# RWKV keys left unnormalised: the inverse squared norm moves into the inversion of the 32x32 blocks

## The chip, the cores and the metric

The kernel runs on one core of one Trainium2 chip. The metric is device time in microseconds (us) of one execution. A core has a matrix engine (TensorE; PE in the profile, with its weight loads shown apart as PEld), a vector engine (VectorE, DVE), a scalar engine (ScalarE, ACT), a general engine (GpSimd, POOL) and SyncE (SP), which here only issues transfers. Transfers are issued by SP and by ACT. Each engine works through its own instructions in a fixed order, so an instruction that waits holds up everything behind it on that engine.

## The reference

The model has two layers on 1024 tokens of width 1024: an even layer (a gated mixer) and an odd layer (RWKV-7 time mixing), each followed by a SwiGLU feed-forward block (FFN). The change lies in the odd layer. What matters of it, cut:

```python
kk = heads(k * k_k)                                   # 16 heads of 64
kk = kk / jnp.maximum(jnp.sqrt(jnp.sum(kk * kk, axis=-1, keepdims=True)), 1e-12)
k = k * (1 + (a - 1) * k_a)
y = wkv7_scan(rh, decay, kh, vh, -kk, kk * ah)
...
def step(state, inp):                                 # one token
    r_t, w_t, k_t, v_t, a_t, b_t = inp                # a_t = -kk, b_t = kk * a
    sa = jnp.einsum('bhvk,bhk->bhv', state, a_t)
    state = (state * w_t[:, :, None, :] + sa[..., None] * b_t[:, :, None, :]
             + v_t[..., None] * k_t[:, :, None, :])
    return state, jnp.einsum('bhvk,bhk->bhv', state, r_t)
```

So each head's key vector `kk` is divided by its length before it enters the recurrence, once as `-kk` and once as `kk * a`.

## The kernel before, in words

Dense products. Every large product is made of three products in a reduced 32-bit format: weights and activations are split into a high and a low part (`split`, L156: ScalarE copies the high part, L157; VectorE subtracts, L158), and `mm3` (L398) multiplies high by high, low by high and high by low into one PSUM tile of 128x512 (L399, L400, L401). "A dense product" below is one of these three. Small products (norms, bonus, interactions, transposes) are made in full 32-bit floats. The tokens are treated in two halves of 512.

The odd layer of a half goes through two stages that concern us.

**Projections** (`project`, L1184). A loop runs over 8 pairs of heads (`p`). For each pair: the 24 dense products of `k`; the decay and learning-rate products (L1291, L1292) with their tanh on ScalarE; the 24 dense products of `r`, among which small products are placed (`small`, L1319). `norms` (L1313) is four products of the squared keys with a two-column indicator (L1314), which leave the squared norms of 512 tokens in columns of the PSUM tile `bo`; then VectorE (L1316) and GpSimd (`rsqrt`, L404) turn them into inverse norms `rn`. After the `r` products, eight products of `rn` with the identity (L1333) spread the inverse norms over the partitions into `rb`, and VectorE multiplies `k * k_k` by it (L1339) to get `kkn`. From `kkn` come `ar` and `bk`, which are stored to DRAM. One pair later, `interact` (L1233) makes 16 products of `bk` with `ar` (L1238), stores their 32x32 diagonal blocks to `at_d`, and after pairs 3 and 7 loads the blocks of four pairs as `iat` (L1253). `bonus` (L1259) adds four small products per pair (L1260).

**Inversion** (`invert`, L1402). For four pairs at once, with one block per partition, VectorE runs 31 steps of two instructions (L1413, L1418) on `xi`, which starts as the identity (L1407, L1408 on GpSimd), then copies (L1420) and stores it to `xi_d` (L1422). The steps are interleaved with the pair loop and with the products of `v` that follow it (L1385 to L1387). A half has two inversions; the second uses the same tiles as the first.

**Recurrence** (`recur`, L1440) of 8 chunks of 64 tokens, emitted beside FFN products that fill TensorE meanwhile (`drive`, L1019). After every second chunk `turn_out` (L1678) transposes the result on TensorE (L1460 from `ysb`), VectorE multiplies it by the gate (L1691), and it is stored to `y_d` (L1694). `take_act` loads `y_d` in four pieces on ScalarE's queue (L121), splits each into `ahi` and `alo`, and `out_proj` (L1726) multiplies them by the output weights.

Order. The program is built with a scheduler (`schedule_with_timeline_sim=True`, L2034): the order of each engine's instructions is fixed when the kernel is built, by a simulated timeline of the whole program with priorities for the recurrence. A small change in one stage therefore moves instructions in those behind it.

PSUM has 8 banks. In the projections they are 3 for dense products, 4 `aux` (for `zw`, `za`, the interactions and `rb`) and 1 `bo` (`PROJ`, L392).

Of the kernel before, what the change touches and what calls it, by code (L numbers as in the profile page):

```python
# [9 lines left out]
F32 = mybir.dt.float32  # L10
# [33 lines left out]
def tile_trunk(  # L44
# [347 lines left out]
    PROJ = {"mm": ("mm", 3), "aux": ("aux", 4), "bo": ("bo", 1)}  # L392
# [10 lines left out]
    def rsqrt(t):  # L403
        pool.tensor_tensor(out=t, in0=t, in1=mhalf[:, : t.shape[1]], op=ALU.pow)  # L404
# [640 lines left out]
    xi_d = [dram.tile([2, 8, 2, 8, 32, 2, 32], F32, name=f"xi_d{h}") for h in range(2)]  # L1045
    at_d = [dram.tile([2, 8, 2, 8, 32, 32], F32, name=f"at_d{h}") for h in range(2)]
# [137 lines left out]
    def project(h, hn1, kp, ring, keep, before_v):  # L1184
# [3 lines left out]
        def tmp(tag, bufs=1, shape=None, dt=F32):  # L1188
            if early.get(tag):
                return early[tag].pop(0)  # L1190
            return ep.tile(shape or [P, HT], dt, tag=tag, bufs=bufs, name=tag)
# [34 lines left out]
        ind2 = tmp("ind2", 1, [P, 2])  # L1226
        pool.memset(ind2, 0.0)
        pool.memset(ind2[0:64, 0:1], 1.0)
        pool.memset(ind2[64:128, 1:2], 1.0)
# [3 lines left out]
        def interact(p, ar, bk):  # L1233

            oa = auxt()
            for c in range(8):
                for r in range(2):
                    pe.matmul(  # L1238
                        oa[rows[r], c * 64 : (c + 1) * 64], bk[rows[r], c, 0, :], ar[rows[r], c, 0, :],
                        start=True, stop=True,  # L1240
                    )
            at = tmp("kkn", 2)
            act.activation(at, oa, AF.Copy)
            for r in range(2):
                for q in range(2):
                    b0 = r * 64 + q * 32
                    sp.dma_start(
                        at_d[h][q, p, r].rearrange("c s t -> s c t"), c64(at)[b0 : b0 + 32, :, q * 32 : q * 32 + 32]
                    )
            if p % 4 == 3:  # L1250
                iat = tmp("iat", 1, [P, 32, 32])
                for q in range(2):
                    sp.dma_start(  # L1253
                        iat[q * 64 : q * 64 + 64].rearrange("b s t -> b (s t)"),
                        at_d[h][q, p - 3 : p + 1].rearrange("p r c s t -> (p r c) (s t)"),
                    )
                return iat
# [19 lines left out]
        for p in range(KT):  # L1277
# [32 lines left out]
            n2 = bo[:, 64 + 8 * p : 72 + 8 * p]  # L1310
            rn = tmp("rn", 2, [P, 4, 2, 8])[:, 0, 0, :]

            def norms(j):  # L1313
                pe.matmul(n2[:, 2 * j : 2 * j + 2], sq[:, j * P : (j + 1) * P], ind2, start=True, stop=True)  # L1314
                if j == 3:
                    dve.tensor_scalar(out=rn, in0=n2[:, 0:8], scalar1=1e-24, scalar2=None, op0=ALU.max)  # L1316
                    rsqrt(rn)

            small = [lambda j=j: norms(j) for j in range(4)]  # L1319
# [10 lines left out]
            rb = auxt()  # L1330
            for j in range(4):
                for r in range(2):
                    pe.matmul(  # L1333
                        rb[rows[r], j * P : (j + 1) * P], bc(rn[:, 2 * j + r : 2 * j + r + 1], [P, 64]), ident,
                        start=True, stop=True,
                    )
            ar, bk = tmp("ar", 2, [P, 8, 2, 64]), tmp("bk", 2, [P, 8, 2, 64])
            kkn = tmp("kkn", 2)
            dve.scalar_tensor_tensor(out=kkn, in0=kt, scalar=col(C_KK + p), in1=rb, op0=ALU.mult, op1=ALU.mult)  # L1339
# [23 lines left out]
        bs = tmp("rn", 2, [P, 4, 2, 8])  # L1363
# [10 lines left out]
        for cb in range(2):  # L1374
            os_ = [(mmt, auxt)[(j + 2 * cb) // 2 % 2]() for j in range(4)]
# [26 lines left out]
    def invert(h, p0, iat, tmp):  # L1402
# [5 lines left out]
        pool.memset(xf[:, 0:2048:65], 1.0)  # L1408
# [629 lines left out]
```

## Time and profile before

| | |
|---|---|
| median of 3 runs | 2454.44 us (2453.6 to 2456.31) |
| span of the profiled execution | 2450.8 us |
| what lies between that span and the median of the runs | 3.6 us |
| TensorE busy | 2369.0 us (97%), 15567 records |
| VectorE, ScalarE, GpSimd busy | 1476.8 us (60%), 935.9 us (38%), 217.1 us (9%) |
| granted TensorE clock, mean | 0.989 |
| projections of half 0, half 1 | about 846 to 1034 us, 1414 to 1610 us |
| recurrence of half 0, half 1 | about 1060 to 1262 us, from about 1626 us on |

The profile was taken on one execution of its own; its span from the first to the last instruction is the base for sums. Its whole time is not listed separately, so a sum is carried to the runs by the 3.6 us. In the timeline a row gives start, duration, engine, line, operation, output and inputs, and how many like instructions were merged. A row of TensorE lasts longer than the distance to the next row, because products are pipelined: the cost of one is read from start to start. A 32-bit float product appears as two records, so a group of four such products reads "x8".

### The profile page before, as it was taken

What the parts mean: (1) busy time and instruction counts of PE and PEld (TensorE: products, weight loads), DVE (VectorE), ACT (ScalarE), POOL (GpSimd) and SP (SyncE); (2) the same over time, 40 slices, a digit from 0 to 9 for tenths busy, and PEclk for the clock granted to TensorE, in tenths of its full rate; (3) what the DMA queues carried; (4) which work ended last, traced back from release to release, by engine and by line L of the source; (5) the groups of instructions that cost most, each with busy time, mean ns of one, the idle gap of its engine ahead of it and who ended that gap; (6) DMA issues with size and microseconds to landing.
All of it is one profiled execution on the core that took longest, in us unless ns stands there. A gap on an engine that the chain in (4) does not pass through costs nothing. (4 is left out here: it accounts for less than half of the span.)

```text
span 2450.8 us, 38190 instructions
## 1 busy us (share of the span) xinstructions
PE 2369.0 (97%) x15567; PEld 1945.9 (79%) x15567; DVE 1476.8 (60%) x2328; ACT 935.9 (38%) x1403; POOL 217.1 (9%) x246
## 2 busy tenths in 40 slices
PE   8999999999899999999999999999999999999998
PEld 6888888888687788778777678777888788888887
DVE  6445766655558758856767947856664446434443
ACT  6233444443114644422335744433232324322223
POOL 0200000000000033101100133201100001000001
PEclk9999999999999999999999999999999999999999
DMA  5114443334655554774435465675433422433231
GB/s 177 52 60 140 153 146 103 113 103 155 252 203 204 165 149 131 226 212 132 129 126 155 160 166 141 186 223 158 143 112 122 129 78 90 150 105 95 86 103 52
DMA packets 406767, 342.17 MB, mean 140 GB/s; under 512 B 78080, under 2 KB 351616, under 8 KB 405824
## 3 DMA queue, kind: packets, MB, share of 16 engines
q10 hardware_dynamic: 266048, 195.33, 26.3%
q1 hardware_dynamic: 140544, 144.41, 18.8%
q8 instruction: 122, 2.00, 0.3%
q14 instruction: 53, 0.43, 0.0%
HBM read 263.07 MB, written 76.61 MB: 139 GB/s over the span
## 5 line engine op out<-in xcount | busy, mean ns | idle before, releaser
L399 PE MATMUL mm<-ahi,whi 128*128 128x512 f32 x1376 | 541.0, 394 | 5.8 <-DVE h L493 3.7
L400 PE MATMUL mm<-alo,whi 128*128 128x512 f32 x1376 | 541.5, 394 | 1.1 <-DVE alo L158 1.1
L401 PE MATMUL mm<-ahi,wlo 128*128 128x512 f32 x1376 | 540.1, 393 | 1.4 <-DVE wlo L158 1.4
L157 ACT ACTIVATE whi<-raw 128x1024 fp32r<-128x1024 f32 (+1 forms) x280 | 282.0, 1013 | 557.4 <-PE mm L400 428.6
L158 DVE TENSOR_TENSOR wlo<-raw,whi 128x1024 fp32r<-128x1024 f32 (+1 forms) x280 | 328.4, 1177 | 246.5 <-ACT whi L157 231.0
L399 PEld LDWEIGHTS mm<-ahi,whi 128*128 128x128 f32 x1376 | 259.0, 188 | 63.1 <-ACT whi L157 6.2
L401 PEld LDWEIGHTS mm<-ahi,wlo 128*128 128x128 f32 x1376 | 259.2, 188 | 58.4 <-DVE wlo L158 2.7
L400 PEld LDWEIGHTS mm<-alo,whi 128*128 128x128 f32 x1376 | 259.3, 188 | 57.7 <-issue 2.5
L493 DVE TENSOR_TENSOR h<-h,mm 128x512 f32<-128x512 f32 x276 | 185.5, 684 | 162.5 <-PE mm L401 161.6
L399 PE MATMUL mm<-hidhi,wdhi 128*128 128x512 f32 x304 | 117.5, 395 | 2.9 <-ACT hidhi L958 2.3
L400 PE MATMUL mm<-hidlo,wdhi 128*128 128x512 f32 x304 | 119.7, 394 | 0.0
L401 PE MATMUL mm<-hidhi,wdlo 128*128 128x512 f32 x304 | 119.0, 391 | 0.0
L730 PE MATMUL mm<-ahi,whi 128*128 128x512 f32 x296 | 115.6, 390 | 0.0
L731 PE MATMUL mm<-alo,whi 128*128 128x512 f32 x296 | 115.2, 389 | 0.0
L732 PE MATMUL mm<-ahi,wlo 128*128 128x512 f32 x296 | 113.6, 389 | 0.0
L157 ACT ACTIVATE wdhi<-raw 128x1024 fp32r<-128x1024 f32 x42 | 43.5, 1058 | 168.0 <-PE mm L400 133.1
L955 DVE TENSOR_TENSOR sg<-sg,mm 128x512 f32<-128x512 f32 x52 | 35.7, 687 | 118.9 <-PE mm L401 118.7
L399 PE MATMUL mm<-hd,dhi 128*128 128x512 f32 x192 | 75.8, 396 | 13.8 <-DMA hd<-hid_d 10.8
L400 PE MATMUL mm<-hd,dhi 128*128 128x512 f32 x192 | 75.9, 395 | 0.0
L401 PE MATMUL mm<-hd,dlo 128*128 128x512 f32 x192 | 74.8, 393 | 0.0
L399 PEld LDWEIGHTS mm<-hidhi,wdhi 128*128 128x128 f32 x304 | 57.3, 189 | 16.0 <-ACT hidhi L958 2.7
L401 PEld LDWEIGHTS mm<-hidhi,wdlo 128*128 128x128 f32 x304 | 57.5, 189 | 11.9
(395 smaller groups left out, 4278.2 us busy)
## 6 DMA issues: line engine op xcount, KB each, us to landing
raw<-in_ffn_w_down_dram ACTq DMA_DIRECT2D x88, 512.0 KB
raw<-in_ffn_w_gate_dram ACTq DMA_DIRECT2D x74, 512.0 KB
raw<-in_ffn_w_up_dram ACTq DMA_DIRECT2D x74, 512.0 KB
hid_d<-hid SPq DMA_DIRECT2D x36, 512.0 KB
hd<-hid_d SPq DMA_DIRECT2D x26, 512.0 KB
raw<-in_ab_w_in_dram ACTq DMA_DIRECT2D x16, 512.0 KB
raw<-in_ab_w_out_dram ACTq DMA_DIRECT2D x16, 512.0 KB
raw<-in_rwkv_w_r_dram ACTq DMA_DIRECT2D x16, 512.0 KB
```

What stands on the lines that cost most here:

```text
L157: act.activation(hi, src, AF.Copy)
L158: (eng or dve).tensor_tensor(out=lo, in0=src, in1=hi.bitcast(F32), op=ALU.subtract)
L399: pe.matmul(o, whi, xhi, start=first, stop=False)
L400: pe.matmul(o, whi, xlo, start=False, stop=False)
L401: pe.matmul(o, wlo, xhi, start=False, stop=last)
L493: dve.tensor_tensor(out=H[h][:, m, :], in0=H[h][:, m, :], in1=o, op=ALU.add)
L730: pe.matmul(o, wh[:, k, :], x[0][:, k, :], start=st, stop=False, skip_group_check=True)
L731: pe.matmul(o, wh[:, k, :], x[1][:, k, :], start=False, stop=False, skip_group_check=True)
L732: pe.matmul(o, wl[:, k, :], x[0][:, k, :], start=False, stop=k == 3, skip_group_check=True)
L955: dve.tensor_tensor(out=s, in0=s, in1=o, op=ALU.mult)
```

## The change

The keys enter `ar` and `bk` as `k * k_k`, without the division. Instead, the blocks that are inverted are multiplied along their columns by the inverse of the squared norm, and the inversion starts from a diagonal of these inverses and not of ones.

- The four small products L1314, the two instructions that follow them and the eight products L1333 are gone. In their place stands one product per pair with the full 512 columns of squared keys; its weights `heads` are zero but for two columns, whose position depends on the pair, so that four pairs add up 8 rows of sums in the PSUM tile `n2`, which takes one of the four `aux` banks.
- After four pairs ScalarE copies the 8 rows out, two transfers store them to `n2_d`, and two bring them into the last row of `iat` (which the inversion does not read), one value per block and token. VectorE takes the maximum with 1e-24, the reciprocal, and multiplies the 31 other rows.
- `kkn` is now made by ScalarE from SBUF (a copy with a scale), and no longer by VectorE from PSUM.
- In `invert`, VectorE copies the inverses onto the diagonal of `xi`; GpSimd wrote ones there before.
- In the last part of the products of `v`, the PSUM tile `n2` serves in place of an `aux` tile.

```diff
-    PROJ = {"mm": ("mm", 3), "aux": ("aux", 4), "bo": ("bo", 1)}
+    PROJ = {"mm": ("mm", 3), "aux": ("aux", 3), "bo": ("bo", 1), "n2": ("n2", 1)}
...
+    n2_d = [dram.tile([2, 8, 2, 8, 32], F32, name=f"n2_d{h}") for h in range(2)]
...
-        ind2 = tmp("ind2", 1, [P, 2])
-        pool.memset(ind2, 0.0)
-        pool.memset(ind2[0:64, 0:1], 1.0)
-        pool.memset(ind2[64:128, 1:2], 1.0)
+        heads = tmp("heads", 1, [P, 6 + P])
+        pool.memset(heads, 0.0)
+        pool.memset(heads[0:64, 6:7], 1.0)
+        pool.memset(heads[64:128, 7:8], 1.0)
+        ind2, sums = heads[:, 6:8], [None]
...
             if p % 4 == 3:
                 iat = tmp("iat", 1, [P, 32, 32])
+                d2 = iat[:, 31, :]
                 for q in range(2):
                     sp.dma_start(
-                        iat[q * 64 : q * 64 + 64].rearrange("b s t -> b (s t)"),
-                        at_d[h][q, p - 3 : p + 1].rearrange("p r c s t -> (p r c) (s t)"),
+                        iat[q * 64 : q * 64 + 64, 0:31].rearrange("b s t -> b (s t)"),
+                        at_d[h][q, p - 3 : p + 1].rearrange("p r c s t -> (p r c) (s t)")[:, : 31 * 32],
                     )
+                    sp.dma_start(
+                        d2[q * 64 : q * 64 + 64], n2_d[h][q, p - 3 : p + 1].rearrange("p r c t -> (p r c) t")
+                    )
+                dve.tensor_scalar(out=d2, in0=d2, scalar1=1e-24, scalar2=None, op0=ALU.max)
+                dve.reciprocal(d2, d2)
+                dve.tensor_tensor(out=iat[:, 0:31], in0=iat[:, 0:31], in1=bc(d2.unsqueeze(1), [P, 31, 32]), op=ALU.mult)
                 return iat
...
-            n2 = bo[:, 64 + 8 * p : 72 + 8 * p]
-            rn = tmp("rn", 2, [P, 4, 2, 8])[:, 0, 0, :]
-
-            def norms(j):
-                pe.matmul(n2[:, 2 * j : 2 * j + 2], sq[:, j * P : (j + 1) * P], ind2, start=True, stop=True)
-                if j == 3:
-                    dve.tensor_scalar(out=rn, in0=n2[:, 0:8], scalar1=1e-24, scalar2=None, op0=ALU.max)
-                    rsqrt(rn)
-
-            small = [lambda j=j: norms(j) for j in range(4)]
+            if p % 4 == 0:
+                sums[0] = pst("n2")
+
+            def norms(p=p, sq=sq):
+
+                k = p % 4
+                pe.matmul(sums[0], heads[:, 6 - 2 * k : 6 + P - 2 * k], sq, start=k == 0, stop=k == 3)
+                if k == 3:
+                    n2 = nt.tile([P, HT], F32, tag="nsq", bufs=2, name="n2")
+                    act.activation(n2[:8], sums[0][:8], AF.Copy)
+                    for q in range(2):
+                        sp.dma_start(
+                            n2_d[h][q, p - 3 : p + 1].rearrange("p r c t -> (p r) c t"),
+                            n2[:8].rearrange("m (c q t) -> m q c t", q=2, t=32)[:, q],
+                        )
+
+            small = [norms]
...
-            rb = auxt()
-            for j in range(4):
-                for r in range(2):
-                    pe.matmul(
-                        rb[rows[r], j * P : (j + 1) * P], bc(rn[:, 2 * j + r : 2 * j + r + 1], [P, 64]), ident,
-                        start=True, stop=True,
-                    )
...
-            dve.scalar_tensor_tensor(out=kkn, in0=kt, scalar=col(C_KK + p), in1=rb, op0=ALU.mult, op1=ALU.mult)
+            act.activation(kkn, kt, AF.Copy, scale=col(C_KK + p))
...
-            os_ = [(mmt, auxt)[(j + 2 * cb) // 2 % 2]() for j in range(4)]
+            os_ = [pst(t) for t in (("mm", "mm", "aux", "aux"), ("aux", "n2", "mm", "mm"))[cb]]
...
-        pool.memset(xf[:, 0:2048:65], 1.0)
+        dve.tensor_copy(xf[:, 0:2048:65], iat[:, 31, :])
```

The scheduler moves instructions at three places of which the prediction speaks.

First, TensorE in a middle pair of half 0, before: the bonus products and the spreading of the inverse norms lie in the `k` products of the next pair, each in one group (`xhi` are the inputs of `k`, `ahi` those of `r`).

```order
L401 MATMUL mm<-xhi,wlo 128x512
L1260 MATMUL bo<-ind_6460,k 128x2 x4
L399 MATMUL mm<-xhi,whi 128x512
...
L1333 MATMUL aux<-ident,rn 64x128 x8
L400 MATMUL mm<-xlo,whi 128x512
...
L1314 MATMUL bo<-ind_6460,kkn 128x2
L1238 MATMUL aux<-ar,bk 64x64 x16
L1314 MATMUL bo<-ind_6460,kkn 128x2 x3
L400 MATMUL mm<-alo,whi 128x512
```

And the same engine in such a pair with the change (line numbers are those of the changed kernel: L1240 are the interactions, L1269 the bonus, L1325 the new full product):

```order
L1240 MATMUL aux<-ar,bk 64x64 x16
L399 MATMUL mm<-ahi,whi 128x512
L400 MATMUL mm<-alo,whi 128x512
L401 MATMUL mm<-ahi,wlo 128x512
L1269 MATMUL bo<-heads,k 128x2
L399 MATMUL mm<-ahi,whi 128x512
L400 MATMUL mm<-alo,whi 128x512
L401 MATMUL mm<-ahi,wlo 128x512
L1269 MATMUL bo<-heads,k 128x2
L1325 MATMUL n_7022<-kkn,heads 128x512
L399 MATMUL mm<-ahi,whi 128x512
L400 MATMUL mm<-alo,whi 128x512
```

The interactions moved from behind 22 `r` products to the front of the `r` products, and the four bonus products of a pair no longer stand in one group: three dense products lie between one and the next.

Second, VectorE with the change, in pair 3 of half 0 (L1360 is `bk`, L1364 and L1365 use the `r` products, L1358 and L1359 finish `k`; `wlo_7027` belongs to the `k` weights of pair 5):

```order
L1360 TENSOR_TENSOR bk_6921<-kkn_6922,em_6875 128x8x64
L1263 TENSOR_SCALAR iat_6324<-iat_6324 128x32
L1364 TENSOR_TENSOR ar_6920<-mm_6880,epx_6876 128x8x64
L1264 RECIPROCAL iat_6324<-iat_6324 128x32
L1358 TENSOR_TENSOR k_6833<-k_6833,av_6867 128x512
L1417 COPY xi_6323<-iat_6324 128x32
L158 TENSOR_TENSOR wlo_7027<-raw_6937,whi_7026 128x1024
L1359 TENSOR_TENSOR bk_6921<-k_6833,em_6875 128x8x64
L1365 SCALAR_TENSOR_TENSOR k_6833<-mm_6880,vec_73,k_6833 128x512
```

The new instruction L1263, which needs the sums back from DRAM, stands ahead of the pair's own work. Before, the first instruction on VectorE that needed a load of `iat` was L1413, the first step of the inversion.

Third, TensorE at the end of the recurrence of half 0, before: the last transposes of the result (from `ysb`), and the first products of the output projection (from `ahi_10851`, which is loaded from `y_d`). Between them lie 84 dense products of the FFN.

```order
L1460 MATMUL sm_10829<-ident_63,ysb_10737 128x128 x4
L400 MATMUL mm_11003<-hidlo_10988,whi_10993 128x512
...
L400 MATMUL mm_11164<-hd_8176,whi_11072 128x512
L401 MATMUL mm_11164<-hd_8176,wlo_11073 128x512
L399 MATMUL mm_11251<-ahi_10851,whi_11078 128x512
L400 MATMUL mm_11251<-alo_10852,whi_11078 128x512
```

With the change (`ahi_10753` is the same input; L434 and later L447 belong to the next norm):

```order
L1469 MATMUL sm_10731<-ident_63,ysb_10639 128x128 x4
L399 MATMUL mm_11019<-hd_8076,whi_10901 128x512
...
L401 MATMUL mm_11066<-hd_8078,wlo_10975 128x512
L399 MATMUL mm_11153<-ahi_10753,whi_10980 128x512
L400 MATMUL mm_11153<-alo_10754,whi_10980 128x512
L401 MATMUL mm_11153<-ahi_10753,wlo_10981 128x512
...
L434 MATMUL aux_11123<-small_70,nacc_11100 128x1 x4
```

Now 30 dense products lie between the last transposes and the first product of the output projection; the other 54 have moved ahead of the transposes. In half 1 a whole block of FFN products still follows the transposes, before and with the change.

More of the change, by code (lines that the diff above doesn't have):

```diff
@@ L1361, in project @@
             bonus(prev[0], prev[3], j)
-        bs = tmp("rn", 2, [P, 4, 2, 8])
+        bs = tmp("rn", 1, [P, 4, 2, 8])
         dve.tensor_copy(bs, bo[:, 0:64].rearrange("t (j p r) -> t j r p", p=8, r=2))
```

## Prediction

> **What bounds the kernel now.** I read the page's busy times first, then the two stretches of the projections, then who waits for whom there.
>
> ```profile
> PE 2369.0 (97%) x15567; PEld 1945.9 (79%) x15567; DVE 1476.8 (60%) x2328; ACT 935.9 (38%) x1403; POOL 217.1 (9%) x246
> ```
>
> ```profile
> 846.00:1034.00 188.00, 179.95 (x1135) 147.55 (x1134) 130.31 (x224) 86.49 (x124) 53.47 (x57) 0.98 0.61 168
> 1414.00:1610.00 196.00, 189.10 (x1180) 155.48 (x1180) 141.70 (x251) 91.34 (x129) 57.26 (x56) 0.99 0.61 168
> ```
>
> The second view gives, per stretch, its length and the busy time of TensorE (PE), its weight loads, VectorE, ScalarE, GpSimd. TensorE is busy 180 of 188 us and 189 of 196; VectorE follows with 130 and 142. So a TensorE instruction taken away here shortens the stretch, as long as what comes later is ready sooner too. The waits of TensorE in the first stretch, and two of the second:
>
> ```profile
> PE aux L1238 <- DVE bk L1351: 2.3, 2, 2.0
> PE mm L1386 <- DVE wlo L158: 2.1, 1, 2.1
> PE mm L399 <- ACT epx L1212: 2.0, 1, 2.0
> PE bo L1260 <- DVE rn L1316: 1.4, 1, 1.4
> ...
> PE aux L1238 <- DVE bk L1351: 2.6, 2, 2.2
> PE bo L1260 <- DVE rn L1316: 1.2, 1, 1.2
> ```
>
> Two rows carry `rn` and two `bk`, both behind the norms that the change rearranges. The spreading products wait a little too (the rows of line L1333 name their releaser, with the time and the count for both halves):
>
> ```profile
>   POOL rn L404: 1.3, 2
> ```
>
> **What the TensorE work costs.** A dense product costs the distance to the next one. The first and last of 115 in a row:
>
> ```profile
> 1034.01 0.39 PE L399 MATMUL mm<-ahi,whi 128*128 128x512 f32 x1
> ...
> 1059.85 0.39 PE L399 MATMUL mm<-ahi,whi 128*128 128x512 f32 x1
> ```
>
> 114 distances in 25.84 us: 0.227 us each. A group set between dense products then costs the time from the dense product before it to the second one after it, less 0.45 us. Four such places: norms alone, spreading alone, bonus with spreading, norms with interactions.
>
> ```profile
> 870.33 0.39 PE L401 MATMUL mm<-xhi,wlo 128*128 128x512 f32 x1
> 870.56 0.95 PE L1314 MATMUL bo<-ind,kkn 128*128 128x2 f32 x8
> ...
> 871.69 0.40 PE L400 MATMUL mm<-alo,whi 128*128 128x512 f32 x1
> ...
> 876.73 0.39 PE L401 MATMUL mm<-ahi,wlo 128*128 128x512 f32 x1
> 877.04 1.09 PE L1333 MATMUL aux<-ident,rn 128*64 128x128 f32 x16
> ...
> 878.40 0.40 PE L1292 MATMUL aux<-twlo,w 128*128 128x512 f32 x1
> ...
> 917.44 0.39 PE L401 MATMUL mm<-xhi,wlo 128*128 128x512 f32 x1
> 917.67 0.95 PE L1260 MATMUL bo<-ind,k 128*128 128x2 f32 x8
> 918.54 1.09 PE L1333 MATMUL aux<-ident,rn 128*64 128x128 f32 x16
> ...
> 919.90 0.40 PE L400 MATMUL mm<-xlo,whi 128*128 128x512 f32 x1
> ...
> 926.73 0.39 PE L399 MATMUL mm<-ahi,whi 128*128 128x512 f32 x1
> 926.95 0.72 PE L1314 MATMUL bo<-ind,kkn 128*128 128x2 f32 x6
> 927.61 1.15 PE L1238 MATMUL aux<-ar,bk 64*64 64x64 f32 x32
> 928.69 0.38 PE L1314 MATMUL bo<-ind,kkn 128*128 128x2 f32 x2
> ...
> 929.25 0.39 PE L401 MATMUL mm<-ahi,wlo 128*128 128x512 f32 x1
> ```
>
> Norms 0.91, spreading 1.22, bonus with spreading 2.01, norms with interactions 2.07. A bonus group has the shape of a norms group (0.91); together with 1.22 that would be 2.13, so two groups side by side save about 0.12: the price of leaving the dense stream and returning. One small product is then (0.91 - 0.12) / 4 = 0.20, interactions alone 2.07 - 0.91 + 0.12 = 1.28, and a small product standing alone 0.32. The new full product has a twin in the even layer, a 32-bit float product with 512 columns:
>
> ```profile
> 94.25 0.39 PE L401 MATMUL mm<-ahi,wlo 128*128 128x512 f32 x1
> 94.48 1.02 PE L635 MATMUL aux<-zq,pw 128*128 128x512 f32 x2
> ...
> 95.57 0.40 PE L400 MATMUL mm<-alo,whi 128*128 128x512 f32 x1
> ```
>
> It costs 1.32 - 0.45 = 0.87. So as a replacement of the four small ones it brings almost nothing; the gain is the spreading.
>
> **The change part by part.** (1) In three pairs of a half (0, 1, 2) I count groups as grouped as before: removed 0.91 + 1.22, added 0.87, saved 1.26 each. In the five others the bonus products now stand one by one, one of them beside the new product: before 2.01 + 2.07 = 4.08, after 1.28 (interactions) + 4 x 0.32 + 0.87 - 0.12 = 3.31, saved 0.77. Per half 3 x 1.26 + 5 x 0.77 = 7.6, in both **15.2 us**. A single bonus product is not in the trace: its floor is the 0.20 it costs in a group, and I take as ceiling half of the full product, 0.43. With 40 of them that moves the sum by +5 or -4 us; 0.32 stands between, since it is a group's switch and body.
>
> By the Trainium skill ("TensorE: Matmul & The Clock Gate", section on LDWEIGHTS) a weight load takes its columns / 1.2 in ns, 107 ns for 128 columns, and a single product of two passes would expose two of them, 0.21 us; by that estimate the saving would be 20 us and not 15. No run here shows a single one yet.
>
> (2) The waits for `rn` go: 1.4 + 1.2, and 1.3 of the spreading, **3.9 us**. The waits for `bk` (4.9 together) have two answers: `bk` no longer comes after norms and spreading, but its reader moved ahead by 22 dense products, 5 us. I take half, **2.4 us**, ends 0 and 4.9.
>
> (3) ScalarE's new copy replaces a VectorE instruction; ScalarE is busy 86 of 188 us, so it hides, and VectorE's few extra instructions per inversion come to less than the 8 it drops. If that cover were gone, they would cost their own length. GpSimd loses the inverse roots and its queue only gets shorter.
>
> (4) The sums go PSUM, ScalarE, DRAM, `iat`. L1263 waits for them at the head of VectorE's queue; behind it stand `ar`, `bk`, a `wlo` that is due a whole pair later, and `k`, which the next bonus needs some 8 us after the `r` products end (24 products 5.4, four decay products 0.9, interactions 1.3, three more 0.7). The nearest round trip through DRAM on SP's queue:
>
> ```profile
> 1007.42 1.93 SPq L1365 DMA_DIRECT2D bon_d<-rn  x1
> 1014.65 1.34 SPq L1367 DMA_DIRECT2D bon<-bon_d  x2
> ```
>
> 7.2 us from issue to the next issue, with other work around it. The new product lies about 5 us before the `r` products end, so L1263 is free some 4 to 5 us after that end, and the seven instructions behind it need about as long again. That just fits; I charge **-1 us**, ends 0 and -8. SP's later stores behind the two new loads wait with them; nobody reads those before the recurrence.
>
> (5) The end of the recurrence in half 0. This is the term that speaks against the change. The way of the result from the last transposes to the output projection:
>
> ```profile
> 1261.43 0.93 PE L1460 MATMUL sm<-ident,ysb 128*128 128x128 f32 x7
> ...
> 1264.39 0.53 SPq L1694 DMA_DIRECT2D y_d<-gch  x1
> ...
> 1267.95 0.33 ACTq L121 DMA_DIRECT2D raw<-y_d  x1
> ...
> 1271.83 1.06 ACT L157 ACTIVATE ahi<-raw 128x1024 fp32r<-128x1024 f32 x1 [11.25 <-DMA raw<-y_d]
> ...
> 1278.11 1.06 ACT L157 ACTIVATE ahi<-raw 128x1024 fp32r<-128x1024 f32 x1 [3.32 <-DMA raw<-y_d]
> ...
> 1281.45 1.06 ACT L157 ACTIVATE ahi<-raw 128x1024 fp32r<-128x1024 f32 x1 [1.24 <-DMA raw<-y_d]
> ...
> 1284.44 1.06 ACT L157 ACTIVATE ahi<-raw 128x1024 fp32r<-128x1024 f32 x1 [1.41 <-DMA raw<-y_d]
> ...
> 1285.53 1.23 DVE L158 TENSOR_TENSOR alo<-raw,ahi 128x1024 fp32r<-128x1024 f32 x1 [0.57 <-ACT ahi L157]
> ```
>
> From the transposes' end (1262.4) the store is issued after 2.0 us and lands 3.6 later; the first piece is there 3.9 after that, later ones 3.0 to 3.3 apart; a split takes 2.3. The last piece is ready 24.4 us after the transposes. Before, 84 dense products (19 us) and the first 18 of the projection's own cover that. With the change three loads go out at once, so I let the pieces arrive at 9.5, 12.8, 16.0 and 19.1 us and the last be split at 21.4; its six products end at 22.8. Without a wait the first 24 products of the projection would end after 30 + 24 dense products (12.2) and the norm's small ones (1.8), at 14.0. So TensorE waits **-8.8 us**, ends 0 (the simulated order, in which nothing waits) and -11.8 (the old 24.4). In half 1 the FFN block covers the whole way, at no cost.
>
> Sum: 15.2 + 3.9 + 2.4 - 1 - 8.8 = 11.7. The span goes from 2450.8 to 2439, and with the 3.6 us that the runs' median lies above it, the runs to **2443 us**.
>
> **The rivals.** *No wait at the output projection* (20%): the four loads, issued without the stops of before, arrive in time. For it: transfers there were slowed by stores of the same moment. Against: one piece alone took 3.9 us. Then 2443 - 8.8 = 2434. *The gain is taken back* (15%): the inversions on VectorE, not TensorE, set when the recurrence starts; TensorE arrives early and waits, the projection for 11.8, `bk` waits stay, L1263 costs 2 more in each half. 2443 + 3.0 + 2.4 + 4 = 2452, no change. For it: the recurrence's start hangs on the last inversion. Against: the interactions come earlier, and so does the first inversion. *Slower* (5%): the sums' round trip. Each of four inversions has L1263 at the head of VectorE's queue; TensorE has some 8 us of cover; once the trip passes about 9 us, every us more is paid four times. At 14 us it costs 20, and the time is 2462. The trace's 7.2 speaks against it.
>
> **How the numbers follow.** My case has 60%, with a range of its own of 2436 to 2449. The range for all, **2431 to 2453**, takes in the case without the wait and most of the case without gain. A measurement here tells 0.2% (5 us) from no change. Faster than 2449.5: the first case all but 5%, the second whole, a quarter of the third, 0.79; slower by as much 0.06; the rest, 0.15, is no change.
>
> **What would show it.** Right: L1325 between dense products costs 0.87 and single bonus products about 0.32; no wait on `rn`; at the end of the first recurrence a wait of L399 or L400 for `ahi` or `alo` of some 9 us in pieces; half 1 shorter than half 0 by that much more. Wrong: waits of the dense products for `wlo` in pair 3, 4 or in the `v` products (L1263 too late), single bonus products near 0.43, or no wait at the projection.

## The result, and the profile after

The changed kernel took 2444.49 us (median of 6 runs, 2442.07 to 2448.9), beside 2455.47 us for the kernel before (6 runs): a ratio of 0.9949 with a 95% interval of 0.9934 to 0.9965, that is 9 to 16 us less. The forecast was 2443 us, in a range of 2431 to 2453. The profiled execution has a span of 2441.4 us, 9.4 less than before's 2450.8. So the number came out nearly as predicted. The places did not.

I cut both executions at five events of TensorE: the first gate product of each half's projections, the last `v` product of each half, and the first product of each recurrence (L1462 before, L1471 after). The view that gives busy time and granted clock per stretch, of the kernel after; columns are from and to, length, TensorE's busy time, granted clock, DMA share, GB/s:

```profile
846.90:1019.50 172.60, 166.16 (x954) 1.00 0.66 181
1019.50:1052.30 32.80, 30.08 (x137) 1.00 0.70 202
1052.30:1391.70 339.40, 324.86 (x3625) 0.97 0.49 148
1391.70:1569.60 177.90, 169.66 (x954) 0.98 0.67 177
1569.60:1609.50 39.90, 34.62 (x156) 1.00 0.73 214
1609.50:2433.10 823.60, 808.32 (x5762) 0.99 0.37 110
```

And the first, fifth and last of the same stretches of the kernel before:

```profile
847.30:1034.00 186.70, 178.65 (x1129) 0.98 0.61 168
...
1594.10:1626.40 32.30, 30.33 (x134) 1.00 0.81 248
1626.40:2442.60 816.20, 806.22 (x5781) 0.99 0.37 112
```

The projections (first and fourth row) became 14.1 and 12.2 us shorter. But half 1 behind its last `v` product became 15.0 us longer (848.5 us before, 863.5 after), and half 0 behind its last `v` product 2.2 us longer. To see what the time is made of, each stretch is taken apart: *idle* is the length less TensorE's busy time, *clock* is half of the time in which TensorE was busy while its granted clock was at 0.5 (the only lowered value in these traces), and *work* is the rest. Low clock during idle time costs nothing and is not counted. In us, before and after, and for one experiment that is told below:

| stretch | before: length (idle, clock, work) | after | after, with the store moved |
|---|---|---|---|
| projections, half 0 | 186.7 (8.0, 3.3, 175.3) | 172.6 (6.4, 0.0, 166.2) | 171.5 (4.2, 1.7, 165.6) |
| to the start of recurrence 0 | 26.5 (0.2, 0.0, 26.3) | 32.8 (2.7, 0.0, 30.1) | 30.0 (0.0, 0.0, 30.0) |
| from there to half 1 | 343.5 (20.1, 3.4, 320.0) | 339.4 (14.5, 8.3, 316.6) | 337.3 (15.6, 4.8, 316.9) |
| projections, half 1 | 190.1 (9.6, 4.7, 175.7) | 177.9 (8.2, 3.3, 166.3) | 177.3 (8.9, 1.7, 166.7) |
| to the start of recurrence 1 | 32.3 (2.0, 0.0, 30.3) | 39.9 (5.3, 0.0, 34.6) | 35.0 (0.0, 0.0, 35.0) |
| from there to the end | 816.2 (10.0, 5.1, 801.1) | 823.6 (15.3, 9.4, 798.9) | 818.0 (13.7, 6.7, 797.6) |
| sum | 1595.3 (49.9, 16.6, 1528.8) | 1586.2 (52.5, 21.0, 1512.7) | 1569.1 (42.5, 14.8, 1511.8) |

TensorE's work fell by 16.1 us: by 18.5 in the projections, against 2.5 more behind them. Of the 16.1, 7.0 are lost again: idle time rose by 2.6, and 4.4 more went to a lower clock. Now the views that answer to those of the prediction. TensorE is busy 2357.0 us in 15215 records, VectorE 1469.6, ScalarE 945.3, GpSimd 177.8.

TensorE's waits after, in the projections of half 0, at the start of recurrence 0, and from 1400 to 1615 us; then before, at the start of recurrence 0 and of recurrence 1 (total, times, longest):

```profile
PE bo L1269 <- DVE k L1365: 3.9, 3, 2.3
PE mm L1395 <- DVE wlo L158: 1.4, 1, 1.4
...
PE sm L1471 <- DMA bk<-bk_d: 2.7, 1, 2.7
...
PE sm L1471 <- DMA bk<-bk_d: 5.3, 1, 5.3
PE bo L1269 <- DVE k L1365: 3.2, 2, 2.4
...
PE sm L1462 <- DMA bk<-bk_d: 0.2, 1, 0.2
...
PE sm L1462 <- DMA bk<-bk_d: 2.0, 1, 2.0
```

No row carries `rn` any more and no interaction waits for `bk`. In their place the bonus products wait 7.1 us for `k`, and the recurrences' first products (L1471) wait 2.7 and 5.3 us for `bk_d`, where before they waited 0.2 and 2.0.

The prices of the new TensorE instructions, from two places of half 0's timeline: the full product, and a single bonus product:

```profile
867.68 0.39 PE L400 MATMUL mm<-xlo,whi 128*128 128x512 f32 x1
867.91 1.02 PE L1325 MATMUL n<-kkn,heads 128*128 128x512 f32 x2
...
869.00 0.40 PE L399 MATMUL mm<-ahi,whi 128*128 128x512 f32 x1
...
903.62 0.39 PE L401 MATMUL mm<-ahi,wlo 128*128 128x512 f32 x1
903.85 0.28 PE L1269 MATMUL bo<-heads,k 128*128 128x2 f32 x2
...
904.30 0.39 PE L400 MATMUL mm<-alo,whi 128*128 128x512 f32 x1
```

The full product costs 869.00 - 867.68 - 0.45 = 0.87 us. A single bonus product costs 904.30 - 903.62 - 0.45 = 0.23; the other undisturbed ones read 0.23 to 0.24, but for two that read 0.33. In all, 44 of them stand alone.

The end of recurrence 0, where the prediction saw its largest loss:

```profile
1268.80 0.39 PE L401 MATMUL mm<-hd,wlo 128*128 128x512 f32 x1
1274.73 0.80 PE L399 MATMUL mm<-ahi,whi 128*128 128x512 f32 x1 [5.54 <-ACT ahi L157]
1275.99 0.80 PE L400 MATMUL mm<-alo,whi 128*128 128x512 f32 x1 [0.46 <-DVE alo L158]
1276.59 0.63 PE L401 MATMUL mm<-ahi,wlo 128*128 128x512 f32 x1
1277.01 0.63 PE L399 MATMUL mm<-ahi,whi 128*128 128x512 f32 x1
```

TensorE waits 5.5 us for `ahi`. After that, dense products follow each other at 0.43 us instead of 0.23. The granted clock (the third number from the right) in the stretches around it says why:

```profile
1262.00:1269.00 7.00, 6.98 (x31) 1.00 0.71 244
1269.00:1274.00 5.00, 0.19 (x1) 0.72 1.00 287
1274.00:1284.00 10.00, 8.80 (x24) 0.50 0.73 242
1284.00:1290.00 6.00, 6.00 (x25) 0.93 0.71 190
```

The clock is halved while TensorE idles and stays so until about 1285, with TensorE at work from 1274.7 on. Of 13.7 us at half clock, 3.5 lie in the wait and cost nothing; the other 10.2 cost 5.1 us, nearly as much as the wait itself. (The expectations of the experiments count the whole as 6.8.) The same happens at the start of recurrence 1: 5.3 us of wait, and from 1609 to 1616 us a granted clock of 0.51 with TensorE at work, 3.3 us lost.

### The profile page after: what moved, and what is told of

It reads as the page before. It is cut to its first block, busy times and chain, and to the rows that moved or that the text cites. A ratio compares the mean times of both kernels' runs of the same rounds, so it can differ in the third digit from the quotient of the medians.

```text
span 2441.4 us, 37434 instructions
## 1 busy us (share of the span) xinstructions
PE 2357.0 (97%) x15215; PEld 1924.3 (79%) x15215; DVE 1469.6 (60%) x2312; ACT 945.3 (39%) x1423; POOL 177.8 (7%) x226
## 4 chain that ended last, share of the span: by engine, by line
PE 75%; DVE 12%; DMA 7%; ACT 3%; issue 2%; SPq 1%; POOL 0%; ACTq 0%; POOLq 0%; DVEq 0%
PE mm L399 16%; PE mm L400 16%; PE mm L401 16%; PE mm L730 5%; PE mm L732 5%; PE mm L731 5%; PE sm L1469 4%; DVE wlo L158 2%; DVE it L1422 1%; DMA bk<-bk_d 1%; PE yp L1469 1%; DVE mix L1172 1%; DVE h L493 1%; DVE xi L1427 1%; DMA raw<-in_ffn_w_down_dram 1%
## 5 line engine op out<-in xcount | busy, mean ns | idle before, releaser
L399 PE MATMUL mm<-ahi,whi 128*128 128x512 f32 x1376 | 551.6, 402 | 7.2 <-ACT ahi L157 5.5
L730 PE MATMUL mm<-ahi,whi 128*128 128x512 f32 x296 | 115.6, 390 | 0.0
L399 PE MATMUL mm<-hd,dhi 128*128 128x512 f32 x192 | 75.8, 396 | 13.7 <-DMA hd<-hid_d 11.9
L401 PEld LDWEIGHTS mm<-hidhi,wdlo 128*128 128x128 f32 x304 | 57.5, 189 | 12.2 <-issue 0.2
```

Of the source, the lines that this page charges most:

```text
L399: pe.matmul(o, whi, xhi, start=first, stop=False)
L401: pe.matmul(o, wlo, xhi, start=False, stop=last)
L730: pe.matmul(o, wh[:, k, :], x[0][:, k, :], start=st, stop=False, skip_group_check=True)
```

## The experiments

Ratios are to the kernel before, measured beside it; times are medians of the same runs. The changed kernel stands at 0.9949 (0.9934 to 0.9965).

**More work at the output projection.** A direct attempt at the low clock: fill the wait.

```diff
     drive(steps_b)
+    spare = mmt()
+    for i in range(24):
+        xh = nxt["hn"][0][:, i % KT, :]
+        pe.matmul(spare, xh[:, :P], xh, start=i == 0, stop=i == 23)
```

> The changed kernel, and 24 full products more that nobody reads (operands from the even layer's input, 24 x 0.227 = 5.4 us of TensorE) between the last down products of half 0 and its output projection, where TensorE waits 5.5 us for ahi and is then granted 0.50 of its clock for 13.6 us. Clock theory: the wait is filled, the clock does not fall, and more work makes the kernel faster: about 6.8 us less than the changed kernel's 2444.5, so near 2438; the granted clock between 1270 and 1286 us is 1.00. Rival, the wait alone costs and the low clock is an accident of that execution: no change, 2444 to 2446. Rival, TensorE has no slack there: slower by up to 5.4, 2450.

It took 2451.16 us, ratio 0.9986 (0.9974 to 0.9997): 6.7 us slower than the change, somewhat more than the 5.4 us of added work; the third expectation is the nearest. The trace shows that the wait did not go but moved; TensorE's two largest waits between 1255 and 1300 us in this kernel:

```profile
PE mm L401 <- DVE wlo L158: 2.7, 1, 2.7
PE aux L434 <- DVE nacc L413: 2.0, 1, 2.0
```

`ahi` is in time now; instead the norm's sums and the output projection's own weights are late, and the clock still falls (0.92 granted from 1255 to 1300 us, some 3.4 us lost). So this run does not test the clock, but it says that the wait there has more than one cause.

**Holding dense products back.** The prediction's term for the output projection rests on 54 dense products that moved ahead of the last transposes. Here the last 120 are held behind the recurrence's last `yp` product.

```diff
-    drive(ffn(0, 1, nxt["hn"], f, D0P[3:], nd=2))
-    drive(steps_b)
+    rest = ffn(0, 1, nxt["hn"], f, D0P[3:], nd=2)
+    for _ in range(24):
+        next(rest)
+    with tc.issue_after(marks[0]):      # marks[0]: the last yp product
+        drive(rest)
+        drive(steps_b)
```

> The changed kernel; of half 0's dense products beside the recurrence the last 120 are held behind the recurrence's last yp product (20 more than the 100 that stand there in the changed kernel), so that more lies between the result's transposes and the output projection. No product is added or left out. Cover theory: the wait for ahi (5.5 us) and the low clock behind it (6.8 us lost) go, the recurrence loses some 2 to 4 us in its last chunk that has no dense product beside it: 9 us less than the changed kernel, about 2435. Rival, the recurrence in half 0 is a chain of waits that dense products only fill: what is taken from it returns as waits of the same length, 2442 to 2446.

It took 2441.93 us, ratio 0.9939 (0.9923 to 0.9956): 2.6 us under the change, within the uncertainty of both. Now 48 dense products lie between the last transposes and the output projection, where the change has 30. The wait there became two short ones (from 1255 to 1300 us: total, times, longest):

```profile
PE mm L399 <- ACT ahi L157: 2.1, 2, 1.5
```

The clock lost between the last transposes and half 1 fell to 1.7 us. Yet recurrence 0 to half 1 took 339.8 us, as in the change (339.4): idle time 15.1 in place of 14.5, clock 6.6 in place of 8.3, work 318.1 in place of 316.6. The rival stands: what is taken from the one place returns in others. The long wait at the output projection is where half 0 shows its slack; that it sets the length isn't seen.

**The store of the second inversion.** SyncE's queue at the start of recurrence 1, in the changed kernel and, last, the same store in the kernel before:

```profile
1596.32 1.12 SPq L1431 DMA_DIRECT2D xi_d<-xi  x2
1597.54 1.80 SPq L1484 DMA_DIRECT2D ar<-ar_d  x1
1599.39 2.14 SPq L1486 DMA_DIRECT2D bk<-bk_d  x1
...
1614.22 1.13 SPq L1422 DMA_DIRECT2D xi_d<-xi  x2
```

The loads of `ar` and `bk`, which recurrence 1 needs first, stand behind the store of `xi`, and that waits for VectorE's second inversion. The last `v` product ended at 1569.6, 26.7 us before that store. In the kernel before, it went out 20.1 us behind the last `v` product (1614.22 and 1594.1). Counted from the first gate product of half 1, the last `v` product comes 12.2 us earlier than before and the store only 5.6; in half 0 it is 14.1 and 8.0. So the faster TensorE has outrun the inversion, by 6.6 and 6.1 us, and the way from the last `v` product to the recurrence became 7.6 and 6.3 us longer. The edit gives that store another queue:

```diff
-            sp.dma_start(
+            (act if p0 else sp).dma_start(
                 xi_d[h][q, p0 : p0 + 4]...
```

> The changed kernel; the second inversion of each half stores its result on ScalarE's DMA queue instead of SyncE's. On SyncE's queue the first loads of the recurrence (ar, bk) stand behind that store, which waits for VectorE until 1038.8 us in half 0 and 1596.3 in half 1. Queue theory: the loads go out earlier, the recurrence starts up to 5 us earlier in each half, the waits for bk_d (2.7 and 5.3 us) and the clock lost behind them (1.7 and 3.4) go; half 0's gain is eaten again at the output projection, half 1's stays: 5 to 10 us less than the changed kernel, 2435 to 2440. Rival, the inversion itself is what the recurrence needs: the wait moves to the products that read XT, 2443 to 2446. Rival, ScalarE's queue is blocked by the store and its weight splits come late: slower by 2 to 5 us.

2426.71 us, ratio 0.9879 (0.9861 to 0.9897): 18 us less than the change, more than expected. In its trace `ar` and `bk` are loaded 11 and 7 us before the store of `xi`, which now is on ScalarE's queue (SyncE's rows, then ScalarE's):

```profile
1580.06 0.34 SPq L1484 DMA_DIRECT2D ar<-ar_d  x1
1583.74 0.34 SPq L1486 DMA_DIRECT2D bk<-bk_d  x1
...
1590.96 1.30 ACTq L1431 DMA_DIRECT2D xi_d<-xi  x2
```

And TensorE has no wait between the last `v` product and the recurrence, in either half:

```profile
1017.90:1047.90 30.00, 30.00 (x133) 1.00 0.77 224
...
1562.50:1597.50 35.00, 35.00 (x155) 1.00 0.76 229
```

By the table above, idle time fell by 10.0 us, lost clock by 6.2 and work by 0.9. Of the idle time, 8.0 us are the waits for `bk_d`. The wait for `ahi` at the output projection is as long as before (5.6 us, with 13.7 us of low clock); it only comes 6.4 us earlier. So the expectation that it would eat half 0's gain was wrong. With the store moved the scheduler also put some 14 of VectorE's instructions in recurrence 1 into another order, so the edit isn't the queue alone there.

**One half at a time.** With the store moved in half 0 alone, TensorE, VectorE and GpSimd issue the same instructions in the same order as in the change.

```diff
-            sp.dma_start(
+            (act if p0 and h == 0 else sp).dma_start(      # the other run: h == 1
```

> The changed kernel with the second inversion's store on ScalarE's queue in half 0 alone; TensorE, VectorE and GpSimd issue exactly the same instructions in the same order as in the changed kernel. With both halves' stores moved the time fell from 2444.5 to 2426.7. If half 0's earlier start of the recurrence is carried to the end: 5 to 7 us less, 2437 to 2440 (the wait of 2.7 us for bk_d, the 1.7 us of clock behind it, and what follows the recurrence). Rival, the wait at the output projection eats it: 2443 to 2446.

> The changed kernel with the second inversion's store on ScalarE's queue in half 1 alone (half 0 in the same order as in the changed kernel). If half 1's start of the recurrence, a wait of 5.3 us and the clock lost behind it, is the larger part of what the change loses: 8 to 12 us less, 2432 to 2437. Rival, the two halves are worth the same, 8 to 9 each; or the gain of both needs both, and this one stays above 2440.

Half 0 alone: 2439.28 us, 0.9926 (0.9903 to 0.9948), 5.2 less than the change. Half 1 alone: 2433.31 us, 0.9900 (0.9878 to 0.9921), 11.2 less. Both are as expected, but half 0's interval overlaps that of the change; half 1's is clear of it. The two add to 16.4, near the 17.8 of both. The late start of the recurrence in half 1 was the larger loss, as its stretch in the table says; the other order of VectorE in recurrence 1 comes with this half's edit alone.

**The same edit in the kernel before.** Does the store's place cost what it does because of the change?

> The kernel before, with the second inversion's store on ScalarE's DMA queue, as in the run that took 18 us from the changed kernel. If the place of that store costs only because the change lets TensorE arrive early: TensorE's waits for bk_d at the recurrences' start were 0.2 and 2.0 us here, so 0 to 4 us less than before's 2455, 2451 to 2455. Rival, the store's place costs as much in any kernel: 2437 to 2440, and then the changed kernel's lost time has another cause than its early arrival.

2449.54 us, ratio 0.9970 (0.9959 to 0.9982): 7.7 less than the 2457.20 us of the kernel before beside it, above what was expected but less than half of what the same edit takes from the changed kernel. So some 10 of the 18 us are there because of the change; by the intervals it may be 3 to 16. Where the other 7.7 come from isn't shown. The waits of 0.2 and 2.0 us for `bk_d` are gone, but the profiled execution is the slowest of its seven (2452.68 us, span 2451.0), while that of the kernel before was a fast one (span 2450.8), so the two don't show the gain: behind the first gate product this one has 5.7 us less idle time, and 5.5 more lost to the clock.

**The sums' way through DRAM.** L1263 now takes its sums from a constant in DRAM, written when the stage begins.

```diff
-    d2[q * 64 : q * 64 + 64], n2_d[h][q, p - 3 : p + 1]...
+    d2[q * 64 : q * 64 + 64], n3_d[h][q, p - 3 : p + 1]...     # n3_d: a constant
```

> The changed kernel, but the inversion takes the sums of squares from a constant that was written to DRAM at the stage's start, so VectorE's L1263 waits for no fresh sums (the sums are still formed and stored, but unread; the keys are scaled by a constant and not normalised). TensorE's and ScalarE's instructions and their order are the same. The prediction's term for the round trip was 1 us (0 to 8): 2442 to 2444.5 by it. Rival, the 13.2 us that VectorE waits at L1263 push the inversions back and with them the recurrences: 6 to 8 us less, 2436 to 2439.

2447.18 us, ratio 0.9961 (0.9948 to 0.9975): no gain. But the edit did not take the wait away; VectorE waits 16.0 us at this instruction (L1269 here), where the change waits 13.2 at L1263. For the first inversion of a half the instruction moved to the start of the half, where it waits 5.0 and 0.0 us for its load; in the change, with fresh sums, it waited only 1.3 and 1.2 there. For the second inversion it waits 3.9 and 7.1 us, as in the change (3.5 and 7.2). SyncE's rows of the change in half 0, from the store of the sums on, then VectorE's row in the change and in this kernel:

```profile
973.51 1.48 SPq L1330 DMA_DIRECT2D n_d<-n  x2
...
990.95 0.50 SPq L1256 DMA_DIRECT2D iat<-at_d  x1
...
995.60 1.95 SPq L1260 DMA_DIRECT2D iat<-n_d  x1
...
1002.83 0.18 DVE L1263 TENSOR_SCALAR iat<-iat 128x32 f32<-128x32 f32 x1 [3.46 <-DMA iat<-n_d]
...
1006.85 0.18 DVE L1269 TENSOR_SCALAR iat<-iat 128x32 f32<-128x32 f32 x1 [3.90 <-DMA iat<-n_d]
```

The last load of the sums goes out 22 us after their store; it stands in SyncE's queue behind the load of the blocks themselves. So in the second inversion it isn't the freshness of the sums that L1263 waits for. What that wait costs stays open.

**The bonus products later.** They waited 7.1 us for `k`; here they come 9 dense products later, where they stood before the change.

```diff
-            small = [norms]
+            small = [norms] + [lambda: None] * 3
```

> The changed kernel with the four bonus products of a pair let into the r products at their fifth to eighth step, where they stood before the change, instead of the second to fifth: 9 dense products, 2 us, later. In the changed kernel they wait 7.1 us for k (longest 2.3 and 2.4). If that wait is a cost of its own: 4 to 6 us less, and the clock that falls behind such waits with it, 2437 to 2441 where the changed kernel takes 2444.5; the waits of the bonus products for k come to 1 or 2 us. Rival, the inversions set the recurrence's start (the store stands 19 us behind the last v product in half 0): TensorE arrives earlier, and the wait for bk_d takes it: 2443 to 2446.

2445.02 us, ratio 0.9959 (0.9944 to 0.9974): no gain, the time that the rival gave. Waits of this kernel in the projections of half 0, and from half 1 on to recurrence 1:

```profile
PE mm L1395 <- DVE wlo L158: 2.5, 1, 2.5
...
PE bo L1269 <- DVE k L1365: 1.1, 1, 1.1
...
PE sm L1471 <- DMA bk<-bk_d: 5.2, 1, 5.2
PE mm L1395 <- DVE wlo L158: 2.5, 1, 2.5
```

The waits for `k` fell from 7.1 to 2.2 us, those for `wlo` rose, and the idle time of the two projections together is the same (14.7 us, 14.6 in the change). The waits for `bk_d` are as long as in the change (2.7 and 5.2), not longer, so the rival's reason was not the right one.

**Both, with the store moved.**

> The changed kernel with the bonus products later, and the second inversion's store on ScalarE's queue, so that the recurrence does not wait for it. If both are costs of their own: 5 us less than the store alone (2426.7), about 2421. Rival, the waits for k hide nothing else and return elsewhere: 2425 to 2428.

> The changed kernel with both edits: the store on ScalarE's queue, and the last 120 dense products of half 0 held behind the recurrence. If the wait at the output projection (5.6 us, and 6.8 us of clock behind it) is still there to be had once the recurrence starts freely: 2418 to 2421. Rival, as in the run with the hold alone, what is taken there returns in the recurrence: 2424 to 2427.

Later bonus products and the moved store: 2424.82 us, 0.9884 (0.9868 to 0.9901). Held dense products and the moved store: 2426.88 us, 0.9873 (0.9858 to 0.9888). Both are level with the moved store alone, so no cost of their own is seen for the waits for `k` or for the wait at the output projection there either.

**The spreading alone.**

```diff
-            rb = auxt()
-            for j in range(4): ...          # 8 products of rn with the identity
-            dve.scalar_tensor_tensor(out=kkn, in0=kt, scalar=col(C_KK + p), in1=rb, ...)
+            dve.scalar_tensor_tensor(out=kkn, in0=kt, scalar=col(C_KK + p), in1=bc(flat, [P, HT]), ...)
```

> The kernel before, without the products that spread the inverse norms (16 groups of 1.22 us); kkn is scaled by a constant instead, so the keys are not normalised, and the norms are still summed and their inverse roots still computed, but unread. In its order 84 dense products stay between half 0's last transposes and the output projection, as before. If the spreading is the whole saving and the cover decides what is left of it: 19.5 us of TensorE and the 3.9 us of waits on rn go, and nothing is lost at the output projection: 2432 to 2436, faster than the change. If instead the recurrence and the inversions take the gain back whatever the cover: 2444 to 2448 like the change.

2427.42 us, ratio 0.9891 (0.9868 to 0.9915): 28 less than before, nearly 5 us below the lower end of what was expected if the spreading is the whole saving. TensorE's work in the two projections is 333.3 us, 17.7 less than before and within 1 us of the change's 332.5. So the spreading is nearly the whole of the change's saving in work; the full product and the single bonus products are about even with the norms that they replace. The profiled executions of this kernel and the change differ by 20.2 us behind the first gate product: 8.0 of idle time (44.5 and 52.5), 10.5 of clock (10.5 and 21.0) and 1.8 of work. This kernel, too, waits for `bk_d` at the start of the recurrences, 0.7 and 4.8 us. So that wait by itself isn't what parts it from the change.

Are the 17 us between the medians the change's own additions, or the start of the recurrence? The same kernel with the store moved was to tell:

> The kernel before without the spreading products (keys scaled by a constant, not normalised), and with the second inversion's store on ScalarE's queue. It prices what the change adds once the recurrence's start is free: without the spreading alone it was 2427.4, with the change and the store moved 2426.7. If the change's own additions (the full product, the single bonus products, L1263 to L1265) cost nothing beyond the start of the recurrence, this one stays level with 2427, within 3 us. Rival, they cost 7 to 10 us in waits and clock wherever the store stands: 2417 to 2421.

2441.70 us, ratio 0.9948 (0.9933 to 0.9963): 14 us *more* than without the moved store, which neither expectation had. The order differs from the first recurrence on. In the kernel without the spreading alone 84 dense products stay between half 0's last transposes and the output projection, as before; the moved store let the scheduler take 54 of them ahead, as the change does. TensorE's largest wait from 1240 to 1300 us in this kernel:

```profile
PE mm L399 <- ACT ahi L157: 5.6, 1, 5.6
```

Recurrence 0 to half 1 takes 346.2 us in place of 335.4 (4.3 more idle, 5.7 more clock), and the wait for `ahi` is there, in a kernel that has none of the change's new instructions. So that order is not made by the new instructions as such. That the 54 products make the 14 us isn't shown: some 200 of VectorE's instructions stand elsewhere too, and where the change has this order and the held products remove it, the time hardly moves. The run doesn't answer its question, because more than one thing moved at once.

## Why the prediction came out right

The terms against what was measured:

| step | predicted | measured |
|---|---|---|
| TensorE's groups | 15.2 gained | 18.5 of work in the two projections |
| waits in the projections | 5.3 gained (3.9 + 2.4 - 1) | 3.0 of idle time, and 4.7 of clock |
| half 0 behind its `v` products | 8.8 lost | 2.2 lost |
| half 1 behind its `v` products | nothing lost | 15.0 lost |
| sum | 11.7 | 9.4, with 0.4 in the even layer |

**Term 1** was right in kind and 3 us short. The full product costs the 0.87 read from its twin. A single bonus product costs 0.24, not 0.32: a price of 0.12 for leaving the dense stream, which I had taken from two groups side by side, is about 0.04 for a group so small (0.24 less the 0.20 of a product within a group). The 40 that were counted, at 0.08 less, are 3.2 us. The Trainium skill ("TensorE: Matmul & The Clock Gate", section on LDWEIGHTS), by which I estimated 0.21 us and a saving of 20 us, was nearer than my middle: the trace has 0.24 and 18.5.

**Term 2**: the waits for `rn` did go. That `k` would be ready for the bonus "just" in time was wrong; the bonus waited 7.1 us. Yet no cost of its own was seen: without most of that wait (the run with the later bonus) the time was the same, since TensorE then stands longer at other places of the projections, for `wlo` among them. The low clock, which the prediction left out altogether, gave 4.7 us here: before, waits such as the 2.13 us for `wlo` at 985 were followed by low clock.

**Term 4**, the wait at L1263, was taken as 1 us, for the sums' round trip. Where the sums are fresh, in the first inversion of a half, VectorE waits 1.3 and 1.2 us; in the second, where the load stands late in SyncE's queue, 3.5 and 7.2. Before, VectorE waited 8.3 us in all at the first steps of the four inversions. What the 13.2 us cost no run could price.

**Term 5** named the right place, the right queue of work and a wait not far from the real one (6.0 measured, 8.8 forecast, and 5.1 of clock that I had not seen). It came whole at the first products and not in pieces: behind the transposes' end the four splits began after 11.6, 13.8, 15.4 and 18.8 us, where I had the pieces arrive at 9.5, 12.8, 16.0 and 19.1. (In the lines of the prediction the first two splits lie 6.3 us apart, not 3.0 to 3.3.) Yet it was hardly a loss. From the start of recurrence 0 to half 1, waits and clock took 23.5 us before and 22.8 after. Before, TensorE's two largest waits from 1262 to 1404 us, behind the last transposes, were these (total, times, longest):

```profile
PE mm L399 <- DVE h L493: 5.2, 4, 2.5
PE mm L399 <- ACT whi L157: 2.3, 3, 1.5
```

In all TensorE idled 9.5 us there before and 8.3 after: the wait for `ahi` took the place of others. Holding dense products back there brought 2.6 us at most. The step that failed is to charge the longest wait of a stretch as a cost without asking what the other waits of the stretch would do.

**The step that is missing** is the start of the recurrence. "In half 1 the FFN block covers the whole way, at no cost" was said of the result's way to the output projection; the way *into* the recurrence was in no term. It was in a rival, to which I gave 15%: the inversions on VectorE, not TensorE, set when the recurrence starts. That is what the traces show, with SyncE's queue as a link: 2.5 and 3.3 us more waiting for `bk_d`, clock lost behind it, and a later recurrence. The 15.0 us of half 1 are 8.6 of idle time (3.3 in front of the recurrence), 4.3 of clock and 2.1 of work. With the store moved half 1 behind its last `v` product is 10.5 us shorter than in the change, and still 4.5 longer than before. The rival's "the `bk` waits stay" was wrong; the interactions no longer wait. Its "no change" was too dark, since TensorE's saving was 3 us larger. The last sign I had named, half 1 shorter than half 0 by what the output projection costs, came out the other way round: half 0 became 11.9 us shorter, half 1 (from its first gate product to the end) 2.8 longer.

So the time was met because errors cancelled, which is luck: 15.0 us that were not charged in half 1, against 6.6 charged too much in half 0 and 5.7 that the projections gave beyond the forecast. What stays open is how much of the 15.0 is the order that came with the earlier start, apart from the store's queue; why the kernel without the spreading loses less with nearly the same wait; and how much of the clock is the change's. From the first gate product on, the lost clock was 10.5 to 25.9 us in the single profiled executions of these fourteen kernels, with no clear tie to their edits beyond the places named.

The version with the store on ScalarE's queue takes 2426.7 us and beats both kernels: 29 us under the kernel before, 18 under the change.

## What to carry to other kernels

Work taken off the busiest engine can be counted to a few us from the distances in the timeline. What is left of it is decided at the next point where that engine meets another one's chain, so follow that chain (here VectorE's inversion) and look at what stands behind it in a transfer queue: loads that need nothing of it may be waiting there. A long wait isn't a cost by itself: of the three waits that an edit to the changed kernel took away or shortened, only the one at the start of the recurrence paid.

## What the runs showed of the hardware

Lost clock comes in pieces, and not every wait brings one. Of the kernel before, two waits from the timeline, and the stretches with them:

```profile
985.26 0.80 PE L1386 MATMUL mm<-wlo,xhi 128*128 128x512 f32 x1 [2.13 <-DVE wlo L158]
...
1074.80 0.28 PE L1460 MATMUL sm<-XT,gt 32*32 32x32 f32 x6 [2.81 <-ACT bkt L1518]
```

```profile
985.00:990.00 5.00, 4.74 (x28) 0.66 0.72 199
1072.00:1080.00 8.00, 5.20 (x66) 1.00 0.51 153
```

Behind the wait of 2.1 us the clock is low for 0.34 x 5 us x 2 = 3.4 us, which costs 1.7; behind the wait of 2.8 us it stays full. In the kernel after, two such pieces (6.8 us) come with the 5.3 us for `bk_d` and four (13.7 us, from about 1271 to 1285) with the 5.5 us for `ahi`. So the length of a wait alone doesn't decide it. The Trainium skill ("TensorE: Matmul & The Clock Gate", part 1 on the clock gate) describes half the clock after an idle window of about 3.4 us, free-running, and the full clock after one busy window. The size of the pieces agrees. Two things differ: a wait of 2.1 us was enough here, and the longest fall went on for 10 us while TensorE was at work.
